# One kernel, four changes of order: first key products around a burst, gate rows earlier, gate dots held in place

## Chip, cores and metric

The kernel runs on one core of a Trainium2 chip, as one program. The metric is the device time of one execution in microseconds. The engines are named as in the profile: PE multiplies matrices, DVE and POOL are the two vector engines, ACT is the activation engine, and SP issues nearly all DMAs, from one queue that it works off in order.

## The reference, cut to what matters

Two layers update 1024 latent tokens (a 16 x 64 grid) of 1024 channels, beside 256 context tokens that share the weights. Each layer modulates its input, mixes it, gates the result and normalises it:

```
silu_c, silu_cc = silu(c), silu(c_ctx)
for i in range(2):
    shift, scale, gate     = split(silu_c  @ w_ada[i] + b_ada[i], 3)
    shift_c, scale_c, gate_c = split(silu_cc @ w_ada[i] + b_ada[i], 3)
    u, uc = h * (1 + scale) + shift, hc * (1 + scale_c) + shift_c
    y, yc = mixer_a(u, uc) if i == 0 else mixer_b(u, uc)
    h = layer_norm(ALPHA * h + gate * y, ln_g[i], ln_b[i])
    if i == 0:
        hc = layer_norm(ALPHA * hc + gate_c * yc, ln_g[i], ln_b[i])
return h
```

`mixer_a` (layer A here) is a windowed attention with 4 key heads for 16 query heads and rotary positions; `mixer_b` (layer B) attends in a neighbourhood of the grid with a learned bias. Both multiply the attention's output by a SiLU gate and by an output matrix. All is float32.

## The kernel before

A float32 product is made of three matmuls: both operands are split into a high and a low part (`uAh` and `uAl`, `wh` and `wl`), and high x high, high x low and low x high are added in PSUM. Channels are cut into 8 tiles of 128, counted by `kt`.

**Start.** For each channel tile, `mod_load` issues the tile's modulation weights (`wada`, two halves of 512 KB), attention weights and the tile of the input (`hraw`, 640 KB). `mod_rows` makes shift and scale of both modulation vectors as rows by 32 small matmuls (line 546, 16 for each half of `wada`) in the PSUM tile `kc`; ACT copies the rows out (line 553); `mod` turns them into columns by two matmuls (line 561) and DVE adds the bias (line 562, tile `adc`). `u_make` scales and shifts the three token chunks (two of 512 latent tokens, one of 256 context tokens; lines 580 to 584), ACT casts the high part (line 588, `uAh`) and DVE subtracts for the low part (line 589, `uAl`). `k_mm` then makes the key products, 12 of 512 columns in the tiles `kps` and 6 of 256 for the context in `kc` (lines 598 to 600), and `v_mm` the value products (lines 608 to 610). The loop over `kt` runs the modulation one tile ahead of the products. For `kt` of 2 and more the 32 row matmuls are one burst, second half first, held together by `tc.keep_in_program_order`; for tile 1 they are two separate halves.

**Order.** Instructions are written in a program order, and a scheduler then moves them on each engine by their priorities and readiness, except those held by `tc.keep_in_program_order`. `merge(att, fill, lead)` writes pieces of attention and pieces of other PE work in turn, by costs given as numbers.

**End of layer A.** The last attention pieces `att` are merged with output products of token tile 0 (`yA0`). Then `gate_rows` runs twice (`gts[:, 0]` for the latent and `gts[:, 1]` for the context gate): eight matmuls against the identity (line 377) that spread a gate column over all partitions into a large PSUM tile, of which two exist, and an ACT copy (line 378). The last six attention pieces follow, and the output tiles.

**Layer B's gate.** `gate_load` loads half a tile of gate weights into `gwB` (one buffer, 256 KB, line 1235) and `gate_dot` multiplies and sums it on DVE (line 1244), 16 times, for eight channel tiles. They are written one after the other into the sub-blocks of heads 1 to 8.

**Last stage.** For each of 8 token tiles `b`: load of `x` (three buffers, from the DRAM tensor `zdd`, layer A's output), `x * vecs[0] + vecs[1]` on POOL (lines 1340 and 1341), load of the attention output `og` for tile `b + 2`, the output products (`out_part`, lines 451 to 453; for tiles 0 and 1 only the last channel tile, read from `o7`, is left), then on DVE `z = y * g1` (line 1355), `z + x` (line 1356) and statistics (line 1357) by halves, the mean and variance (lines 459 and 460), the power -1/2 on POOL (line 461), two scalings on DVE (lines 1362 and 1364) and the store of the output (line 1365). `g1` is layer B's gate, made by `gate_rows` in the pass of tile 0.

Of the kernel before, what the change touches and what calls it, by code (L numbers as in the profile page):

```python
# [15 lines left out]
ALU = mybir.AluOpType  # L16
# [66 lines left out]
def build(tc, i, out):  # L83
# [452 lines left out]
    def mod_rows(kt):  # L536

        ws = wada.pop(kt)

        burst = kt > 1  # L540
        for n, hf in enumerate((1, 0) if burst else (0, 1)):
            for r in range(2):
                for x in range(2):
                    for kh in range(2):
                        g = 32 * (2 * x + kh)
                        ins = mm(
                            kc[g : g + 32, 512:640], sil[:, 4 * hf + 2 * r + kh, :], ws[hf][:, 2 * r + kh, x * P : (x + 1) * P],
                            start=n + r == 0, stop=n + r == 2, tile_position=(0, g),
                        )
                        if burst and n + r + x + kh:  # L550
                            tc.keep_in_program_order(ins)
        rows[kt] = pp.tile([P, P], F32, tag="rows", bufs=2, name="rows")
        ins = nc.scalar.copy(rows[kt], kc[:, 512:640])
        if kt == 2:

            tc.keep_in_program_order(ins)
# [34 lines left out]
    def k_mm(kt):  # L591
        for c, (t0, n) in enumerate(CHUNKS):
            for nt in range(2):
# [4 lines left out]
                mm(pt, hi[:, sl], rh, start=kt == 0 and (c < 2 or nt == 0), stop=False)  # L598
                mm(pt, lo[:, sl], rh, start=False, stop=False)
                mm(pt, hi[:, sl], rl, start=False, stop=kt == KT - 1 and (c < 2 or nt == 1))  # L600
# [13 lines left out]
    for kt in range(-1, KT + 1):  # L614
        if kt + 1 < KT:
            for n in range(3) if kt < 0 else (kt + 3,) if kt + 3 < KT else ():
                mod_load(n, upto[n])
                if n == 0:
                    w.split(2)
            mod_rows(kt + 1)  # L620
        if kt > 0:
            k_mm(kt - 1)
        if kt + 1 < KT:
            mod(kt + 1)
        if kt < 0:
# [4 lines left out]
        if kt < KT and kt >= 0:  # L630
            u_make(kt)
# [229 lines left out]
    for p in range(8):  # L861
# [13 lines left out]
        else:  # L875
# [22 lines left out]
            merge(att[:-6], fill, lead=1500.0)  # L898
            gts = up.tile([P, 2, D], F32, tag="l2", bufs=1, name="gates")
            for v in range(2):  # L900
                gate_rows(gts[:, v], dcol[:, 0:8, v])
# [335 lines left out]
    def gate_dot(j, x):  # L1237
# [6 lines left out]
        nc.vector.tensor_tensor_reduce(t, t, g, 0.5, acc if x else 0.0, ALU.mult, ALU.add, accum_out=acc)  # L1244
# [89 lines left out]
    for b in range(8):  # L1334
# [11 lines left out]
        parts = [slice(*c) for c in zip(cuts, cuts[1:])]  # L1346
        for sl in parts:
            out_part(y, sl, pairs, woB, range(KT) if b > 1 else (KT - 1,))
        if b == 0:
            g1 = ob.tile([P, D], F32, name="g1")  # L1350
            gate_rows(g1, dcol[:, 24:32, 0])
# [111 lines left out]
```

## Time and profile before

| what | value |
|---|---|
| median of 3 runs | 1423.81 us (1423.17 to 1426.17) |
| profiled execution, its own time | 1422.99 us |
| span of the profiled execution | 1421.2 us |
| granted TensorE clock, mean | 0.997 of full speed |
| PE busy | 1385.3 us (97%) |
| DVE busy | 980.0 us (69%) |
| ACT busy | 731.4 us (51%) |
| POOL busy | 626.2 us (44%) |

The profile shows one execution of the program; its times are counted from the start of the span, which ends 1.8 us short of the execution's own time. Busy time counts an engine's instructions; idle time ahead of one is put down to what ended it. A transfer that is issued from SP's queue starts no earlier than all issues ahead of it there.

### The profile page before, as it was taken

To read this page: it belongs to the slowest core of one execution; us is meant where nothing else is said; L and a number is where in the kernel's file an instruction comes from. 1 tells how busy PE (TensorE), PEld (TensorE's weight loads), DVE (VectorE), ACT (ScalarE), POOL (GpSimd) and SP (SyncE) were. 2 spreads that over 40 slices of the span, in tenths; PEclk is the share of its full clock that TensorE was granted. 3 is DMA by queue.
4 is the path that set the end of the run, shared out by engine and by line. 5 is a ranking of instruction groups with operands and counts; after the bars stand their busy time and mean duration, and the time that the engine had idled before them with its cause. 6 is when DMAs were issued, how large, how long until landed. Compare 5 with 4: busy or idle time off the path is not lost. (4 is left out here: it accounts for less than half of the span.)

```text
span 1421.2 us, 25164 instructions
## 1 busy us (share of the span) xinstructions
PE 1385.3 (97%) x8816; PEld 1215.2 (86%) x8816; DVE 980.0 (69%) x2220; ACT 731.4 (51%) x1560; POOL 626.2 (44%) x776
## 2 busy tenths in 40 slices
PE   8999999999999999999999999999999999999996
PEld 6988898888988888888898899888998899888885
DVE  4658887878888789566433766566665564659598
ACT  4337776676776778432222555454454454558200
POOL 0326676667666567233211333332233232325583
PEclk9999999999999999999999999999999999999998
DMA  9572114123222114443187575564555564476753
GB/s 377 181 224 85 54 57 126 53 79 92 79 73 64 57 60 146 127 135 133 62 260 218 156 214 165 143 189 137 179 150 172 150 185 146 137 209 185 181 149 107
DMA packets 128141, 202.39 MB, mean 142 GB/s; under 512 B 9744, under 2 KB 66448, under 8 KB 128016
## 3 DMA queue, kind: packets, MB, share of 16 engines
q1 hardware_dynamic: 127872, 200.78, 47.0%
q8 instruction: 70, 1.15, 0.3%
q14 instruction: 55, 0.45, 0.1%
q10 hardware_dynamic: 144, 0.01, 0.0%
HBM read 145.18 MB, written 55.57 MB: 141 GB/s over the span
## 5 line engine op out<-in xcount | busy, mean ns | idle before, releaser
L334 POOL TENSOR_SCALAR s_B<-s_B,rs_B 128x640 f32<-128x640 f32 (+1 forms) x128 | 103.2, 806 | 289.8 <-DVE rs_B L333 262.7
L212 PE MATMUL pj<-uBh,wh 128*128 128x512 f32 (+1 forms) x448 | 175.9, 393 | 0.0
L213 PE MATMUL pj<-uBl,wh 128*128 128x512 f32 (+1 forms) x448 | 170.3, 380 | 0.0
L214 PE MATMUL pj<-uBh,wl 128*128 128x512 f32 (+1 forms) x448 | 170.1, 380 | 0.0
L329 ACT ACTIVATE s_B<-s_B,m_B 128x640 f32<-128x640 f32 (+1 forms) x128 | 102.9, 804 | 126.1 <-DVE m_B L322 125.9
L329 ACT ACTIVATE s_A<-s_A,m_A 128x641 f32<-128x641 f32 (+2 forms) x160 | 119.5, 747 | 82.9 <-DVE m_A L322 60.1
L168 POOL TENSOR_TENSOR wl<-wr,wh 128x512 fp32r<-128x512 f32 x65 | 88.2, 1358 | 158.1 <-ACT wh L163 146.4
L334 POOL TENSOR_SCALAR s_A<-s_A,rs_A 128x640 f32<-128x640 f32 (+2 forms) x160 | 128.8, 805 | 65.0 <-DVE rs_A L333 58.9
L322 DVE CUSTOM_DVE_ANT_0 s_A<-S_A,msk,nsk 128x640 f32<-128x640 f32 (+2 forms) x160 | 123.5, 774 | 32.3 <-PE S_A L755 18.2
L347 DVE TENSOR_TENSOR pt_B<-T_B,pt_B 128x640 fp32r<-128x640 f32 (+1 forms) x128 | 100.9, 788 | 60.2 <-ACT pt_B L345 59.7
L212 PE MATMUL pj<-uAh,wh 128*128 128x512 f32 (+1 forms) x384 | 140.2, 365 | 0.8 <-DVE otmp L794 0.8
L213 PE MATMUL pj<-uAl,wh 128*128 128x512 f32 (+1 forms) x384 | 137.6, 358 | 0.0
L214 PE MATMUL pj<-uAh,wl 128*128 128x512 f32 (+1 forms) x384 | 137.2, 357 | 0.0
L347 DVE TENSOR_TENSOR ptl_A<-T_A,pth_A 128x640 fp32r<-128x640 f32 (+2 forms) x160 | 114.1, 713 | 16.8 <-PE pvA L783 10.5
L341 PE MATMUL T_A<-ident,s_A 128*128 128x128 f32 x672 | 100.9, 275 | 10.7 <-DVE m_A L322 5.3
L345 ACT CAST pt_B<-T_B 128x640 fp32r<-128x640 f32 (+1 forms) x128 | 84.4, 659 | 48.2 <-PE T_B L341 47.2
L341 PEld LDWEIGHTS T_A<-ident,s_A 128*128 128x128 f32 x672 | 77.3, 140 | 37.0 <-issue 10.1
L322 DVE CUSTOM_DVE_ANT_0 s_B<-S_B,bias 128x640 f32<-128x640 f32 (+1 forms) x128 | 100.2, 783 | 8.0 <-PE S_B L1092 7.0
L345 ACT CAST pth_A<-T_A 128x640 fp32r<-128x640 f32 (+2 forms) x160 | 96.3, 602 | 17.2 <-PE T_A L341 15.7
L214 PEld LDWEIGHTS pj<-uBh,wl 128*128 128x128 f32 x448 | 84.3, 188 | 16.6
L213 PEld LDWEIGHTS pj<-uBl,wh 128*128 128x128 f32 x448 | 84.7, 189 | 9.1
L341 PE MATMUL T_B<-ident,s_B 128*128 128x128 f32 x608 | 88.1, 274 | 4.2 <-DVE pt_B L347 2.3
(224 smaller groups left out, 3866.8 us busy)
## 6 DMA issues: line engine op xcount, KB each, us to landing
kB<-kdB SPq DMA_DIRECT2D x64, 320.0 KB, 5.4
gw<-in_wadaT SPq DMA_DIRECT2D x48, 256.0 KB, 2.8
vdB<-st SPq DMA_DIRECT2D x20, 512.0 KB, 3.6
vB<-vdB SPq DMA_DIRECT2D x16, 640.0 KB, 4.6
wada<-in_wadaC SPq DMA_DIRECT2D x16, 512.0 KB, 9.6
kdB<-st SPq DMA_DIRECT2D x16, 512.0 KB, 2.8
qdB<-st SPq DMA_DIRECT2D x16, 512.0 KB, 3.7
qB<-qdB SPq DMA_DIRECT2D x32, 256.0 KB, 4.8
```

The source lines that it names most:

```text
L168: e.tensor_tensor(lo, r, f32(hi), ALU.subtract)
L212: mm(pt[:, :n], hi[:, sl], rh, start=kt == 0, stop=False)
L213: mm(pt[:, :n], hi[:, sl], rl, start=False, stop=False)
L214: mm(pt[:, :n], lo[:, sl], rh, start=False, stop=kt == KT - 1)
L322: nc.vector.tensor_tensor_reduce(outp, sc, in1, scale, init if init is not None else 3e38, ALU.add, ALU.min, accum_out=s.m)
L329: nc.scalar.activation(s.t[:, :n], s.t[:, :n], AF.Exp, bias=s.m, scale=-1.0, accum_out=s.sum)
L334: nc.gpsimd.tensor_scalar(s.t[:, : s.w], s.t[:, : s.w], s.rs, 1.0, ALU.mult, ALU.mult)
L341: nc.tensor.transpose(tp[:, k * P : (k + 1) * P], s.t[:, src * P : (src + 1) * P], ident)
L345: nc.scalar.copy(pt.hi[:, :n, hl, :], tv)
L347: nc.vector.tensor_tensor(pt.lo[:, :n, hl, :], tv, f32(pt.hi[:, :n, hl, :]), ALU.subtract)
```

## The change

Four orders are changed, and no arithmetic:

- **Start.** The burst now begins with tile 1, whose 32 row matmuls run together, second half first, all held in program order. Tile 0's scaling is written ahead of tile 1's modulation; of tile 0's 18 key products the first 2 are written ahead of the burst, 4 behind it, and the other 12, the 6 context products among them, behind tile 1's line 561, the last two groups held in program order.
- **End of layer A.** `merge` gets all but the last eight attention pieces; the gate row of the latents, two attention pieces, the gate row of the context, and the last six pieces follow.
- **Layer B's gate.** The 16 dots are held in program order.
- **Last stage.** `gate_rows` is written ahead of tile 0's output products instead of behind them.

```diff
--- before.py
+++ after.py
@@ -537,7 +537,7 @@
 
         ws = wada.pop(kt)
 
-        burst = kt > 1
+        burst = kt > 0
         for n, hf in enumerate((1, 0) if burst else (0, 1)):
             for r in range(2):
                 for x in range(2):
@@ -547,7 +547,7 @@
                             kc[g : g + 32, 512:640], sil[:, 4 * hf + 2 * r + kh, :], ws[hf][:, 2 * r + kh, x * P : (x + 1) * P],
                             start=n + r == 0, stop=n + r == 2, tile_position=(0, g),
                         )
-                        if burst and n + r + x + kh:
+                        if kt == 1 or burst and n + r + x + kh:
                             tc.keep_in_program_order(ins)
         rows[kt] = pp.tile([P, P], F32, tag="rows", bufs=2, name="rows")
         ins = nc.scalar.copy(rows[kt], kc[:, 512:640])
@@ -588,16 +588,21 @@
             nc.scalar.copy(hi, x)
             nc.vector.tensor_tensor(lo, x, f32(hi), ALU.subtract)
 
-    def k_mm(kt):
+    def k_mm(kt, which=slice(None), fixed=False):
+        ps = []
         for c, (t0, n) in enumerate(CHUNKS):
             for nt in range(2):
                 hi, lo = w.got[KEYS[2 * (kt // 4) + nt]]
                 sl = slice((kt % 4) * P, (kt % 4 + 1) * P)
                 rh, rl = uA.at(kt, slice(t0, t0 + n))
                 pt = kps[c, nt] if c < 2 else kc[:, nt * C : nt * C + C]
-                mm(pt, hi[:, sl], rh, start=kt == 0 and (c < 2 or nt == 0), stop=False)
-                mm(pt, lo[:, sl], rh, start=False, stop=False)
-                mm(pt, hi[:, sl], rl, start=False, stop=kt == KT - 1 and (c < 2 or nt == 1))
+                ps.append((pt, hi[:, sl], rh, dict(start=kt == 0 and (c < 2 or nt == 0), stop=False)))
+                ps.append((pt, lo[:, sl], rh, dict(start=False, stop=False)))
+                ps.append((pt, hi[:, sl], rl, dict(start=False, stop=kt == KT - 1 and (c < 2 or nt == 1))))
+        for p in ps[which]:
+            ins = mm(*p[:3], **p[3])
+            if fixed:
+                tc.keep_in_program_order(ins)
 
     def v_mm(kt):
         hi, lo = w.got[VALUES[kt // 2]]
@@ -617,18 +622,27 @@
                 mod_load(n, upto[n])
                 if n == 0:
                     w.split(2)
+            if kt == 0:
+
+                u_make(0)
+                k_mm(0, slice(0, 2))
             mod_rows(kt + 1)
-        if kt > 0:
+            if kt == 0:
+                k_mm(0, slice(2, 6), True)
+        if kt > 1:
             k_mm(kt - 1)
         if kt + 1 < KT:
             mod(kt + 1)
+        if kt == 0:
+            k_mm(0, slice(6, None), True)
         if kt < 0:
 
             warm(vps[:, 0:512], 12)
         if kt > 0:
             v_mm(kt - 1)
         if kt < KT and kt >= 0:
-            u_make(kt)
+            if kt:
+                u_make(kt)
             w.split(upto[min(kt + 1, 7)])
     dma(ident, i["ident"])
     dma(lnc, i["lnc"])
@@ -895,10 +909,12 @@
             fill.append((0.0, og_first))
             for n in range(2 * KT):
                 fill.append((300.0, lambda n=n: out_part(yA0, HALVES[n // KT], oA0, woA, (n % KT,))))
-            merge(att[:-6], fill, lead=1500.0)
+
+            merge(att[:-8], fill, lead=1500.0)
             gts = up.tile([P, 2, D], F32, tag="l2", bufs=1, name="gates")
-            for v in range(2):
-                gate_rows(gts[:, v], dcol[:, 0:8, v])
+            gate_rows(gts[:, 0], dcol[:, 0:8, 0])
+            merge(att[-8:-6], [])
+            gate_rows(gts[:, 1], dcol[:, 0:8, 1])
             raw = og_load(1)
             merge(att[-6:], [])
     px_st.close()
@@ -1241,7 +1257,10 @@
             nc.scalar.activation(t, g, AF.Tanh, scale=0.5)
             nc.vector.scalar_tensor_tensor(g, t, 1.0, g, ALU.add, ALU.mult)
             return
-        nc.vector.tensor_tensor_reduce(t, t, g, 0.5, acc if x else 0.0, ALU.mult, ALU.add, accum_out=acc)
+
+        tc.keep_in_program_order(
+            nc.vector.tensor_tensor_reduce(t, t, g, 0.5, acc if x else 0.0, ALU.mult, ALU.add, accum_out=acc)
+        )
         if j == KT - 1 and x:
             nc.vector.tensor_tensor(dcol[:, 24:32, 0], dcol[:, 24:32, 0], bad[:, 40:48], ALU.add)
 
@@ -1344,11 +1363,12 @@
 
         cuts = (0, 512, 768, 1024) if b == 7 else (0, 512, D)
         parts = [slice(*c) for c in zip(cuts, cuts[1:])]
+        if b == 0:
+
+            g1 = ob.tile([P, D], F32, name="g1")
+            gate_rows(g1, dcol[:, 24:32, 0])
         for sl in parts:
             out_part(y, sl, pairs, woB, range(KT) if b > 1 else (KT - 1,))
-        if b == 0:
-            g1 = ob.tile([P, D], F32, name="g1")
-            gate_rows(g1, dcol[:, 24:32, 0])
         z = ob.tile([P, D], F32, tag="z", bufs=3, name="z")
         st = ob.tile([P, 3, 6], F32, tag="stat", bufs=2, name="stat")
         for j, sl in enumerate(parts):
```

**PE at the start.** The list begins with the first key product of tile 0 and shows the row matmuls of tile 1 (line 546; x8 here is x16 in the profile). In the names, `kp_0` and `kp_1` are the two key column groups, and `uAh_104`, `uAh_105` and `uAh_106` the first and second latent chunk and the context. Before:

```order
L598 MATMUL kp_0_142<-uAh_104,wh_160 128x512
L599 MATMUL kp_0_142<-uAh_104,wl_161 128x512
L546 MATMUL kc<-wada,sil 32x128 x8
L600 MATMUL kp_0_142<-uAl_107,wh_160 128x512
L598 MATMUL kp_1_143<-uAh_104,wh_164 128x512
L599 MATMUL kp_1_143<-uAh_104,wl_165 128x512
L600 MATMUL kp_1_143<-uAl_107,wh_164 128x512
L546 MATMUL kc<-wada,sil 32x128 x8
L598 MATMUL kp_0_144<-uAh_105,wh_160 128x512
L599 MATMUL kp_0_144<-uAh_105,wl_161 128x512
L561 MATMUL kc<-bad,rows 128x4
```

After (key products now stand in line 603):

```order
L603 MATMUL kp_0_142<-uAh_104,wh_160 128x512
L603 MATMUL kp_0_142<-uAh_104,wl_161 128x512
L546 MATMUL kc<-wada,sil 32x128 x16
L603 MATMUL kp_0_142<-uAl_107,wh_160 128x512
L603 MATMUL kp_1_143<-uAh_104,wh_164 128x512
L603 MATMUL kp_1_143<-uAh_104,wl_165 128x512
L603 MATMUL kp_1_143<-uAl_107,wh_164 128x512
L561 MATMUL kc<-bad,rows 128x4
L603 MATMUL kp_0_144<-uAh_105,wh_160 128x512
L603 MATMUL kp_0_144<-uAh_105,wl_161 128x512
L603 MATMUL kp_0_144<-uAl_108,wh_160 128x512
```

The second half of the row matmuls has moved up by four key products, and line 561 by two; behind these rows stand the rest of tile 0's 512-column products, and in the order after directly behind them its six context products, which in the order before follow only behind tile 2's burst.

**DVE at the gate dots.** Before, the dots stand in a row among the first head's softmax; here the fifth and sixth pair of loads (line 1244 is the dot and the read of its sum; line 347 makes `pt_B`, the transposed probabilities for PE):

```order
L333 RECIPROCAL rs_B_9343<-sum_B_9342 128x1
L1244 ISA gwB_1_10801,dcol<-gwB_1_10801,gsil,dcol 128x512
L1244 ISA dcol 128x1
L333 RECIPROCAL rs_B_9359<-sum_B_9358 128x1
L322 ISA s_B_9381,m_B_9382<-S_B_9376,bias_8695 128x640
L322 ISA m_B_9382 128x1
L333 RECIPROCAL rs_B_9384<-sum_B_9383 128x1
L1244 ISA gwB_0_10991,dcol<-gwB_0_10991,gsil 128x512
L1244 ISA dcol 128x1
L347 TENSOR_TENSOR pt_B_9394<-T_B_9395,pt_B_9394 128x4x128
```

After, the first dot stands here (line 1262), some 60 rows further on than the first before:

```order
L322 ISA s_B_9712,m_B_9713<-S_B_9707,bias_8696 128x640
L322 ISA m_B_9713 128x1
L996 SCALAR_TENSOR_TENSOR st<-pj_1_9646,st 128x512
L333 RECIPROCAL rs_B_9715<-sum_B_9714 128x1
L1154 TENSOR_TENSOR otmp<-pvB_2_9725,otmp 64x256 x2
L1262 ISA gwB_0_9656,dcol<-gwB_0_9656,gsil 128x512
L1262 ISA dcol 128x1
L347 TENSOR_TENSOR pt_B_9763<-T_B_9764,pt_B_9763 128x4x128
L168 TENSOR_TENSOR wl_9797<-wr_9554,wh_9796 128x512
```

The 16 dots are now spread over heads 1 to 8, behind an addition into `otmp` and ahead of a `pt_B` as here.

**SP in the last stage.** From tile 3's load of `x` on, before:

```order
L1336 DMA x<-zdd 128x1x1024
L1365 DMA out_h<-z 16x8x1024
L395 DMA og<-ogdB 128x4x128 x2
L395 DMA og<-ogdB 128x3x128 x2
L1336 DMA x<-zdd 128x1x1024
L1365 DMA out_h<-z 16x8x1024
L1336 DMA x<-zdd 128x1x1024
```

After:

```order
L395 DMA og<-ogdB 128x3x128
L1385 DMA out_h<-z 16x8x1024
L395 DMA og<-ogdB 128x3x128
L1355 DMA x<-zdd 128x1x1024
L395 DMA og<-ogdB 128x4x128 x2
L395 DMA og<-ogdB 128x3x128 x2
L1385 DMA out_h<-z 16x8x1024
L1355 DMA x<-zdd 128x1x1024 x2
```

The load of `x` for tile 3 (the first here) has moved behind tile 0's output, and that of tile 4 behind tile 1's output, where tile 5's stood already. On PE, tile 0's eight gate matmuls (line 377) have moved up by six products (lines 451 to 453).

## Rows read from the trace of the kernel before

**Rows 1.** The page's first part: engine, busy time, share of the span, instructions.

```profile
PE 1385.3 (97%) x8816; PEld 1215.2 (86%) x8816; DVE 980.0 (69%) x2220; ACT 731.4 (51%) x1560; POOL 626.2 (44%) x776
```

**Rows 2.** Stretches of the span (start:end, length, then for each engine its busy time and, in brackets, its instructions; granted TensorE clock as a share of full speed; DMA share; GB/s).

```profile
60.00:100.00 40.00, 40.00 (x266) 36.93 (x266) 26.59 (x41) 12.57 (x26) 16.59 (x13) 1.00 0.66 204
700.00:800.00 100.00, 98.57 (x591) 86.71 (x590) 41.16 (x98) 30.93 (x61) 19.15 (x19) 1.00 0.68 202
800.00:1200.00 400.00, 399.77 (x2691) 365.26 (x2690) 241.48 (x580) 199.58 (x412) 125.63 (x149) 1.00 0.58 167
1380.00:1421.00 41.00, 30.30 (x154) 25.30 (x152) 34.60 (x47) 0.00 (x0) 17.22 (x10) 0.91 0.41 109
```

**Rows 3.** The waits of PE, for the tile that waits and for what: us in total, times, longest us.

```profile
PE kp L598 <- ACT uAh L588: 2.5, 2, 1.9
PE T_B L341 <- DVE pt_B L347: 2.3, 5, 0.9
```

**Rows 4.** PE's timeline from 11 to 22 us: start, length, engine, line, operation, tile out<-in, shape, count, and in brackets the idle time ahead of it with what ended it.

```profile
11.34 0.50 PE L598 MATMUL kp<-uAh,wh 128*128 128x512 f32 x1 [1.93 <-ACT uAh L588]
...
12.00 0.65 PE L546 MATMUL kc<-wada,sil 128*32 128x128 f32 x16
...
13.14 0.40 PE L599 MATMUL kp<-uAh,wl 128*128 128x512 f32 x1
13.38 0.39 PE L600 MATMUL kp<-uAl,wh 128*128 128x512 f32 x1
13.70 0.64 PE L546 MATMUL kc<-wada,sil 128*32 128x128 f32 x16
...
16.73 0.50 PE L598 MATMUL kp<-uAh,wh 128*128 128x512 f32 x1 [0.58 <-ACT uAh L588]
...
19.00 1.08 PE L546 MATMUL kc<-wada,sil 128*32 128x128 f32 x32
...
20.93 0.28 PE L598 MATMUL kc<-uAh,wh 128*128 128x256 f32 x1
...
21.64 0.28 PE L561 MATMUL kc<-bad,rows 128*128 128x4 f32 x2
```

**Rows 5.** The same stretch on ACT (the casts of tile 1) and on DVE (tile 1's scale and shift).

```profile
16.08 1.43 ACT L588 CAST uAh<-hraw 128x512 fp32r<-128x512 f32 x3
...
15.16 0.16 DVE L562 TENSOR_TENSOR adc<-kc,bad 128x4 f32<-128x4 f32 x1 [2.21 <-PE kc L561]
```

**Rows 6.** The load of the modulation weights: first the DMA view of two short stretches with one such issue in each (4.0 to 4.5 us, tile 1's second half; 11.2 to 12.5 us, tile 3's second half): KB each, us from issue to landing; then SP's issue of the latter.

```profile
wada<-in_wadaC SPq DMA_DIRECT2D x1, 512.0 KB, 7.9
...
wada<-in_wadaC SPq DMA_DIRECT2D x1, 512.0 KB, 10.9
...
11.94 0.33 SPq L528 DMA_DIRECT2D wada<-in_wadaC  x1
```

**Rows 7.** The end of layer A's attention, 574 to 579 us, on PE, then ACT, then DVE.

```profile
574.38 1.04 PE L377 MATMUL gate<-ident,dcol 128*128 128x128 f32 x8
...
576.47 1.09 PE L377 MATMUL gate<-ident,dcol 128*128 128x128 f32 x8
...
578.65 0.50 PE L451 MATMUL yA<-woAh,og 128*128 128x512 f32 x1 [0.88 <-ACT gates L378]
...
577.59 1.01 ACT L378 COPY gates<-gate 128x1024 f32<-128x1024 f32 x1 [0.35 <-PE gate L377]
...
575.98 0.42 DVE L347 TENSOR_TENSOR ptl_A<-T_A,pth_A 128x256 fp32r<-128x256 f32 x1 [3.36 <-PE pvA L783]
```

**Rows 8.** Layer B's gate dots: of the view of the tile gwB the second halves' dots (durations min/median/max in ns, first and last start) and the total wait ahead of the dots (us, times); then the timeline from 786 to 793 us, DVE's rows and PE's.

```profile
L1244 DVE CUSTOM_DVE_ANT_0 gwB<-gwB,gsil,dcol x8: 732/751/1206, 765.9 to 836.1; 128x512 f32<-128x512 f32 x8
...
  DMA gwB<-in_wadaT: 16.5, 12
...
786.88 0.69 DVE L1244 CUSTOM_DVE_ANT_0 gwB<-gwB,gsil 128x512 f32<-128x512 f32 x1 [0.99 <-DMA gwB<-in_wadaT]
...
790.38 1.21 DVE L1244 CUSTOM_DVE_ANT_0 gwB<-gwB,gsil,dcol 128x512 f32<-128x512 f32 x1 [0.30 <-DMA gwB<-in_wadaT]
...
788.33 0.74 PE L341 MATMUL T_B<-ident,s_B 128*128 128x128 f32 x5 [0.94 <-DVE pt_B L347]
...
792.48 0.73 PE L341 MATMUL T_B<-ident,s_B 128*128 128x128 f32 x5 [0.49 <-DVE pt_B L347]
```

**Rows 9.** The last stage: PE's start on tile 0's products behind the gate; two DVE scalings of tiles of the same shape, one beside a POOL operation and one with POOL idle; SP's issues of tile 4's x and of tile 1's output; the DMA view of the stretch with tile 5's x (KB, us to landing); then pieces of the chain that ended last (start, length, what).

```profile
1342.61 0.50 PE L451 MATMUL yB<-woBh,og 128*128 128x512 f32 x1 [0.42 <-DVE z L1355]
...
1350.46 3.41 DVE L1364 SCALAR_TENSOR_TENSOR z<-z,rsd,vec 128x1024 f32<-128x1024 f32 x1
...
1408.33 1.29 DVE L1364 SCALAR_TENSOR_TENSOR z<-z,rsd,vec 128x1024 f32<-128x1024 f32 x1 [0.44 <-POOL rsd L461]
...
1358.30 0.55 SPq L1336 DMA_DIRECT2D x<-zdd  x1
1365.37 0.59 SPq L1365 DMA_DIRECT2D out_h<-z  x1
...
x<-zdd SPq DMA_DIRECT2D x1, 512.0 KB, 5.8
...
1368.70 2.37 POOL x L1340
...
1388.81 5.28 DMA x<-zdd
```

More of the change, by code (lines that the diff above doesn't have):

```diff
@@ L1346, in build @@
         parts = [slice(*c) for c in zip(cuts, cuts[1:])]
-        for sl in parts:
-            out_part(y, sl, pairs, woB, range(KT) if b > 1 else (KT - 1,))
         if b == 0:
@@ L1351, in build @@
             gate_rows(g1, dcol[:, 24:32, 0])
+        for sl in parts:
+            out_part(y, sl, pairs, woB, range(KT) if b > 1 else (KT - 1,))
         z = ob.tile([P, D], F32, tag="z", bufs=3, name="z")
```

## The prediction

> **What bounds the kernel now.** I read the page's first part, then stretches, PE's waits, and last the timelines of the four places that the change touches. PE is busy 1385.3 us [rows 1] of a span of 1421.2, so it sets the time nearly everywhere, and a microsecond is to be won only where PE stands idle or where the last stage ends later than PE does. The stretches show where that is: none from 60 to 100 us, 1.43 us from 700 to 800, 0.23 us in the 400 us from 800 to 1200, and 10.7 us from 1380 on [rows 2], where PE has finished and DVE and POOL bring the last tiles to their end. Two of PE's waits stand in the way of this change: 2.5 us for the first casts `uAh` and 2.3 us for `pt_B` [rows 3]. A gain that reaches PE at 16 us is kept at least up to 100 us, since PE has no idle time from 60 to 100 that could swallow it [rows 2]. At the very end it counts only if DVE's and POOL's chain moves with it.
>
> **Start.** No matmul is added or taken away. Before, PE makes the first half of tile 1's row matmuls at 12.00 us and the second at 13.70 [rows 4], DVE has shift and scale at 15.16, ACT begins the casts at 16.08 [rows 5], and PE waits 0.58 us until 16.73 for the first of them [rows 4]. Now the 32 matmuls stand together. A burst of 32 takes 1.01 us, from 19.00 to the next product; a 512-column product follows the one before it after 0.24 (13.14 to 13.38); a context product takes (21.64 - 20.93) / 6 = 0.12 [rows 4]. So: burst 12.0 to 13.0, four products and a switch to 14.05, line 561 there instead of at about 14.85 (its result came at 15.16 [rows 5], 0.3 later). The scale comes 0.8 us earlier, at 14.36, the first cast, which was ready just ahead of 16.73, at about 15.9. PE meanwhile has six products of tile 0 (6 x 0.24 = 1.4) and six context products (0.7), to about 16.3. The 0.58 us wait is covered, and one switch between row matmuls and products falls away: the two halves took 12.57 - 12.00 and 14.27 - 13.70, 1.14 us together by the starts of what follows, against 1.01, and each return to products costs a longer first one, so I count 0.3 to 0.5. Together about -1.0 to -1.2.
>
> The loads cap it. The burst begins with the half that is loaded last. That half is issued at about 4.1 and lands 7.9 later [rows 6], at 12.0: no margin. Should it come at 13.70, where it was used before [rows 4], a gain of 0.3 is left. Tile 3's second half is issued at 11.94 and takes 10.9 [rows 6], to 22.84, while its burst would start at about 22.7: 0.15 us go back. I take **-1.0**, range -0.3 to -1.4.
>
> **End of layer A.** Before, the eight gate matmuls start at 574.38 and the second eight at 576.47, after DVE's 575.98; ACT's second copy runs from 577.59 to 578.60, and the output product waits 0.88 us for it [rows 7]. That product needs the second large PSUM tile, so it still follows the second copy. Now two attention pieces stand between the two, and PE has four 256-column products and two transposes more to do before that product: 4 x 0.12 [rows 4] and some 0.2, about 0.7 us, which hides most of the 0.88. Against it stands that the attention ahead is merged with fewer pieces in reserve, so a wait for DVE or POOL may show up earlier. I take **-0.5**; the ends are -0.9, all of the wait and no more, and +0.7, a new wait of the size of the one removed less what is won.
>
> **Gate dots.** Before, the 16 dots follow one another from about 762 to 836 us, and DVE, which works in order, waits 16.5 us ahead of them for the loads of `gwB` [rows 8]. Two such places reach PE: the dot at 786.88, which waited 0.99, and the one at 790.38, which ran 1.21; behind them `pt_B` is late and PE waits 0.94 and 0.49 [rows 8], together the 1.43 that PE lost from 700 to 800 [rows 2]. Now each dot stands in a sub-block of its own and its load some two sub-blocks ahead, so DVE should find it loaded. The two waits go: **-1.3**, at most -1.43. What the change adds is that each of the 16 dots, 0.69 or 0.75 long, stands directly ahead of a `pt_B`. The nearest rows: dots run up to 836.1 [rows 8], and PE loses 0.23 us in all from 800 to 1200 [rows 2]. The dots from 800 to 836 therefore cost PE nothing or almost nothing, and I count the new ones at zero too; the other end is a rival below. The loads are the same 16, spread over heads, and free SP.
>
> **Last stage.** Gate matmuls move up by six products, 6 x 0.24 = 1.4 us. PE's wait of 0.42 on DVE's first `z` [rows 9] goes, and DVE starts 1.4 us sooner. But PE does not end the kernel there: the chain runs through POOL's work on `x` at 1368.70, tile 4's, and the load of tile 7's `x` at 1388.81 [rows 9]. In SP's queue, tile 4's `x` was issued at 1358.30, ahead of tile 1's output at 1365.37 [rows 9]; with tile 5's 5.8 us to landing it was there at 1364.1, 4.6 us ahead of POOL. Now it is issued only behind that output. With DVE 1.4 us sooner the output goes at about 1364.0, 0.6 for its issue, and tile 5's load, the nearest, took 5.8; the one on the chain 5.3. That makes 1369.9 with the shorter time (1370.4 with the longer), against 1368.70: POOL, and with it the end, is **1.2** late, while PE's gain of the three earlier places moves all of this stage alike. Bounds: -0.4, if POOL is not the last here and 0.42 of PE's wait counts, and +3, if a DVE step falls behind POOL as well.
>
> **Sum.** -1.0 - 0.5 - 1.3 + 1.2 = -1.6 us. Against the profiled execution's 1422.99 that is 1421.4. That execution is 0.82 us below the median of the three runs, 1423.81; the forecast for the median is 1423.81 - 1.6 = **1422.2**.
>
> **Rivals.** *The last stage gives nothing back.* DVE is early by more than 1.4 us, or POOL waits for DVE in any case, so that tile 4's `x` is in time. Then -2.8, and up to -1.4 more if the whole lead of the gate reaches the end: 1419.6 to 1421.0. For it: the three gains each have a wait of PE that is seen in the rows. Against it: the 1.2 comes from an order in SP's queue that is fixed, and tile 4's load has only 1365.37 - 1358.30 = 7.1 us less room than before.
>
> *The dots hold PE up (slower than before).* Each dot delays a `pt_B` by 0.7, and PE's output products of that sub-block wait for it as they did at 788.33. DVE sits idle a good part of the time from 800 to 1200 (241 of 400 us busy [rows 2]), which speaks against it; that 0.94 of wait arose behind a single dot speaks for it [rows 8]. At 0.4 each, 16 x 0.4 = 6.4 on top of the sum: +4.8, 1428.6. It decides the sign from 1.6 / 16 = 0.1 us for each dot.
>
> *DVE falls behind POOL in the last stage.* The scaling of line 1364 took 3.41 us beside POOL's work on `x` and 1.29 with POOL idle [rows 9], so one such meeting costs 2.1 us. POOL's and DVE's meetings all shift when DVE starts 1.4 sooner and tile 3's and 4's `x` come later. One more meeting on the chain gives -1.6 + 2.1 = +0.5: 1424.3; one fewer gives -3.7: 1420.1, inside the first rival. The Trainium skill, "SBUF — State Buffer", section "SBUF: two separate sides", states it as a rule: a DVE operation with two SBUF inputs and a POOL operation need one shared pair of ports, and whoever starts first keeps it for the whole instruction. By that rule the cost of a meeting is all of the rest of POOL's operation, not a share; the two durations agree with it.
>
> *The change does less than it says.* `wada`'s half lands at 13.7 and the gate rows of layer A only move their wait: -0.3 - 1.3 + 1.2 = -0.4, 1423.4.
>
> **Chances.** The forecast 0.42; nothing given back 0.32; dots 0.10; one more meeting 0.11; less than it says 0.05. A measurement of this kernel tells a change from none from about 0.2% on, 2.85 us: below 1420.96 or above 1426.66. The forecast, the additional meeting and the last case lie within it, 0.58, less 0.01 for a run of them above. The first rival is almost all below, 0.32. The dots and that rest are above, 0.11. The range leaves out the dots, and little at the other end: 1419.4, just below the first rival's lower end, to 1425.5, the meeting with 1.2 more.
>
> **What the next profile would show.** Start: row matmuls x32 at about 12.0, the scale about 0.8 us sooner, no wait of PE for `uAh` behind 11.34. If the burst starts later than 12.3, the load binds. Layer A: an output product behind the second gate copy with a wait under 0.4. Dots: no wait of DVE for `gwB` and none of PE for `pt_B` near 788 and 792; PE waits for `pt_B` in heads 1 to 8 beyond 1 us in all would be the dots' price. Last stage: PE's first product of tile 2 without a wait, but POOL waiting for a load of `x` ahead of tile 4's line 1359; if POOL doesn't wait there, the 1.2 is wrong, and the kernel is faster than I say. If PE's total idle time ahead of 1300 us falls by less than 2 us, the three gains are wrong.

## The result and the profile after

The changed kernel takes 1427.90 us (median of 10 runs, 1425.45 to 1429.88) against 1423.89 for the kernel before (10 runs): ratio 1.0026, 95% interval 1.0017 to 1.0036, or 3.7 us slower (2.4 to 5.1). Its profiled execution took 1427.96 us with a span of 1425.9, 4.7 more than before.

Stretches of the changed kernel, columns as in [rows 2]:

```profile
520.00:580.00 60.00, 56.26 (x366) 49.05 (x366) 47.89 (x108) 46.43 (x99) 36.44 (x54) 1.00 0.36 115
700.00:800.00 100.00, 100.00 (x599) 88.19 (x598) 36.31 (x83) 30.81 (x61) 19.41 (x20) 1.00 0.60 180
800.00:1200.00 400.00, 398.23 (x2678) 363.49 (x2677) 246.37 (x591) 197.86 (x408) 126.04 (x147) 1.00 0.59 172
1380.00:1425.80 45.80, 30.88 (x156) 25.76 (x154) 34.57 (x47) 0.00 (x0) 19.92 (x10) 0.88 0.37 97
```

And one stretch of the kernel before that [rows 2] don't have:

```profile
520.00:580.00 60.00, 58.05 (x378) 50.72 (x377) 48.18 (x114) 47.03 (x102) 38.11 (x55) 1.00 0.36 116
```

Idle time of PE is length less busy time. From 60 to 100 us there is none, as before. From 700 to 800 us it is gone (1.43 before, [rows 2]), but 1.77 us have come from 800 to 1200 (0.23 before), and 520 to 580 has 3.74 where it had 1.95. Busy time in all is the same, 1385.3 us. PE's last product begins 0.58 us later than before (1410.60 against 1410.02), so the rest of the 4.7, some 4.1 us, lies behind PE in this execution: from the last product to the end of the span it is 15.3 us, before 11.2. Ahead of 1300 us PE is idle for 23.9 us, before 22.7; a fall of less than 2 us was the prediction's sign that its three gains are wrong.

PE's timeline at the start, columns as in [rows 4]:

```profile
11.42 0.50 PE L603 MATMUL kp<-uAh,wh 128*128 128x512 f32 x1 [1.80 <-ACT uAh L588]
...
12.13 1.08 PE L546 MATMUL kc<-wada,sil 128*32 128x128 f32 x32
...
14.18 0.28 PE L561 MATMUL kc<-bad,rows 128*128 128x4 f32 x2
...
16.50 0.40 PE L603 MATMUL kp<-uAh,wh 128*128 128x512 f32 x1
...
18.43 1.08 PE L546 MATMUL kc<-wada,sil 128*32 128x128 f32 x32
```

The burst is one, the modulation's matmul (line 561) stands at 14.18, and the first product of tile 1 at 16.50 waits for nothing, where [rows 4] had 0.58. Tile 2's burst starts 0.57 earlier, with one product of 0.24 less and six of 0.12 more done by then. PE has run 529 products by 60 us instead of 521.

PE's timeline at the end of layer A:

```profile
532.75 0.74 PE L341 MATMUL T_A<-ident,s_A 128*128 128x128 f32 x5 [0.94 <-DVE m_A L322]
...
553.05 0.74 PE L341 MATMUL T_A<-ident,s_A 128*128 128x128 f32 x5 [0.71 <-POOL s_A L334]
...
555.95 0.74 PE L341 MATMUL T_A<-ident,s_A 128*128 128x128 f32 x5 [0.50 <-DVE m_A L322]
...
579.83 0.50 PE L451 MATMUL yA<-woAh,og 128*128 128x512 f32 x1 [0.28 <-ACT gates L378]
```

The wait behind the second gate copy fell from 0.88 [rows 7] to 0.28. But waits of 0.5 to 0.9 stand 24 to 47 us ahead of it.

A gate dot, the `pt_B` behind it, and PE's new waits for `pt_B`; DVE's rows first, then PE's:

```profile
983.25 1.45 DVE L1262 CUSTOM_DVE_ANT_0 gwB<-gwB,gsil,dcol 128x512 f32<-128x512 f32 x1
...
984.63 0.81 DVE L347 TENSOR_TENSOR pt_B<-T_B,pt_B 128x640 fp32r<-128x640 f32 x1
...
985.59 0.74 PE L341 MATMUL T_B<-ident,s_B 128*128 128x128 f32 x5 [0.49 <-DVE pt_B L347]
...
1049.20 0.74 PE L341 MATMUL T_B<-ident,s_B 128*128 128x128 f32 x5 [0.36 <-DVE pt_B L347]
```

No dot waits for its load any more. One dot took 1.45 us where the others of its kind take 0.74, and the `pt_B` behind it kept PE waiting 0.49. The other wait has no dot next to it.

The last stage: POOL's rows, then SP's issues of `x` for tile 3 and for tiles 4 and 5:

```profile
1360.83 1.52 POOL L461 TENSOR_TENSOR rsd<-rsd,half 128x1 f32<-128x1 f32 x1 [3.21 <-DVE rsd L460]
1364.36 2.40 POOL L1359 TENSOR_TENSOR x<-x,vec 128x1024 f32<-128x1024 f32 x1 [2.00 <-DMA x<-zdd]
...
1371.38 2.81 POOL L1359 TENSOR_TENSOR x<-x,vec 128x1024 f32<-128x1024 f32 x1 [0.77 <-DMA x<-zdd]
...
1356.73 1.71 SPq L1355 DMA_DIRECT2D x<-zdd  x1
...
1364.46 2.25 SPq L1355 DMA_DIRECT2D x<-zdd  x2
```

POOL waits 3.21 us for DVE ahead of tile 1's power (line 461), then 2.00 and 0.77 for loads of `x`. Tile 3's load was issued at about 1357.9 behind tile 0's store, where before it went at 1346.29, and tile 4's at 1364.46 instead of 1358.30 [rows 9].

### The profile page after: what moved, and what is told of

The parts are those of the page before. It is cut to its first block, busy times and chain, and to the rows that moved or that the text cites. A ratio compares the mean times of both kernels' runs of the same rounds, so it can differ in the third digit from the quotient of the medians.

```text
span 1425.9 us, 25160 instructions
## 1 busy us (share of the span) xinstructions
PE 1385.3 (97%) x8816; PEld 1215.5 (85%) x8816; DVE 979.6 (69%) x2220; ACT 730.7 (51%) x1560; POOL 627.9 (44%) x776
## 5 line engine op out<-in xcount | busy, mean ns | idle before, releaser
L347 DVE TENSOR_TENSOR ptl_A<-T_A,pth_A 128x640 fp32r<-128x640 f32 (+2 forms) x160 | 114.2, 714 | 15.3 <-PE pvA L797 7.4
L212 PEld LDWEIGHTS pj<-uBh,wh 128*128 128x128 f32 x448 | 84.5, 189 | 9.1
```

Source lines behind the costliest of these rows:

```text
L212: mm(pt[:, :n], hi[:, sl], rh, start=kt == 0, stop=False)
L347: nc.vector.tensor_tensor(pt.lo[:, :n, hl, :], tv, f32(pt.hi[:, :n, hl, :]), ALU.subtract)
```

## The experiments

Each was timed beside the kernel before on the same chip, 8 to 11 runs each. Microseconds are the ratio less one, times the median of the kernel before beside it (1424.86 to 1425.71), with the 95% interval.

**The four parts alone.** Each kernel is the one before with one part of the diff.

> Only the start is changed. Theory 1 (the four parts add up, each as far as its own stage shows it after the change): about -0.7 us, which is what the full change shows at 60 us, kept to the end: some 1423.2. Theory 2 (a gain at the start is swallowed later, because waits of layer A follow DVE and POOL): 0 within 0.3 us.

Measured: 0.9996, -0.6 us (-1.9 to +0.7). Neither theory is excluded by the time alone.

> Only the end of layer A is changed. Theory 1: slower by 1.5 to 2 us: the new waits for scores and probabilities between 532 and 560 us cost about 2.6, the wait behind the second gate copy falls from 0.9 to 0.3. Theory 2 (these waits come from the start's shift and not from the earlier end of the merge): -0.6 us, no wait of more than 0.5 us between 532 and 560.

Measured: 1.0024, +3.4 us (+2.3 to +4.7). PE's waits between 520 and 562 us are the ones of the full change.

> Only the 16 gate dots are held in place. Theory 1: about 0 (-1.4 from 786 to 793 us, +1.5 from new waits of 0.2 to 0.7 us in heads 2 to 8). Theory 2 (the dots are what slows the kernel): +2 us or more. My prediction's own step: -1.3.

Measured: 0.9991, -1.3 us (-2.6 to -0.1). In its profile the 1.43 us from 700 to 800 are gone, and PE waits for `pt_B` 0.20, 0.49 and 0.23 us between 947 and 1048. A further wait of 0.80 for scores at 885 is no price of the dots: with the last stage's part alone one of 0.43 stands there too.

> Only the gate rows of the last stage are moved ahead. Theory 1 (tile 3's and 4's loads of x stand behind output stores in SP's queue and POOL waits for them): +3 to +4.5 us, POOL waiting 1 us or more for tiles 3 and 4, PE's last product no later than before. Theory 2 (the loss in the full change comes from the phase in which PE reaches the last stage, after the other three parts): within 1 us of before. My prediction's own step: +1.2.

Measured: 1.0011, +1.6 us (+0.4 to +2.8). The four add up to +3.1; the full change has +3.7. Each has an interval of about 1.3 us either way, so these runs show no action of the parts on each other and would miss a small one. The end of layer A is the largest.

**The end of layer A, taken apart.** First the cut of the merge without moving the gate rows apart:

```diff
-            merge(att[:-6], fill, lead=1500.0)
+            merge(att[:-8], fill, lead=1500.0)
+            merge(att[-8:-6], [])
```

> The kernel before with the merge at the end of layer A cut at eight attention pieces instead of six, and nothing else: the two pieces follow, then both gate rows together, as before. Theory 1 (the cut is what costs: with fewer attention pieces for the same output work, merge writes the output work, and DVE's splits of its weights, earlier between the pieces, and DVE's score maxima come late all the way back to 520 us): slower by 3 us or more, with the waits for m_A between 520 and 562 us and also the 0.9 us behind the second gate copy. Theory 2 (the gate rows apart are what costs): within 0.7 us of before.

Measured: 1.0012, +1.7 us (+0.4 to +3.0). In its profile, ACT's rows, then DVE's, then PE's:

```profile
530.31 0.62 ACT L367 CAST woAh<-wor 128x512 fp32r<-128x512 f32 x1 [1.30 <-DMA wor<-in_wAo]
530.83 0.83 ACT L329 ACTIVATE s_A<-s_A,m_A 128x641 f32<-128x641 f32 x1
...
531.78 0.16 DVE L333 RECIPROCAL rs_A<-sum_A 128x1 f32<-128x1 f32 x1 [1.00 <-ACT s_A L329]
531.90 0.88 DVE L322 CUSTOM_DVE_ANT_0 s_A<-S_A,msk,nsk 128x640 f32<-128x640 f32 x1
...
532.94 0.74 PE L341 MATMUL T_A<-ident,s_A 128*128 128x128 f32 x5 [0.97 <-DVE m_A L322]
```

And ACT in the kernel before, the exponential of the same place and the cast that waits for its load:

```profile
530.43 0.83 ACT L329 ACTIVATE s_A<-s_A,m_A 128x641 f32<-128x641 f32 x1
...
533.85 0.62 ACT L367 CAST woAh<-wor 128x512 fp32r<-128x512 f32 x1 [0.74 <-DMA wor<-in_wAo]
```

After the cut, a cast of output weights (line 367) stands ahead of the exponential, and waits 1.30 us for its DMA. ACT works in order: the exponential's maximum is there at 529.10, and it still begins only behind the cast, at 530.83. DVE's reciprocal (line 333) waits 1.00 for that exponential, the score maximum behind it is late, and PE waits 0.97 for the maximum. In the kernel before, the exponential goes first and the cast that waits comes 3 us later. The cut gives `merge` fewer attention pieces for the same fill, so all fill, the weight casts with it, is written earlier between them, tens of microseconds ahead of the place that the change is about. At this place PE's wait grows from 0.45 to 0.97, which is a part of the 2.9 us that the cut costs by the profile (below). The other new waits, the largest 0.73 at 553.3 for POOL and 0.51 at 556.2, were not taken apart; ahead of the first, splits of output weights (line 368) run on DVE (1.84 us from 550.47) and on POOL (1.32 from 550.45). No run holds such a step back alone: that the cut costs is shown by times, that it does so through these steps is read from the profile.

Then the gate rows apart without the cut, as a piece of no cost inside the merge:

```diff
-            merge(att[:-6], fill, lead=1500.0)
-            for v in range(2):
-                gate_rows(gts[:, v], dcol[:, 0:8, v])
+            first = (0.0, lambda: gate_rows(gts[:, 0], dcol[:, 0:8, 0]), 0)
+            merge(att[:-8] + [first] + att[-8:-6], fill, lead=1500.0)
+            gate_rows(gts[:, 1], dcol[:, 0:8, 1])
```

> The kernel before with the first gate row written two attention pieces earlier, as a piece of no cost inside the merge, so that the merge's other pieces keep their order; only the gate rows move. Theory 1: -0.4 to -0.9 us: the wait behind the second gate copy falls from 0.9 to 0.3 or less, and the waits between 520 and 562 stay as before (0.5 us). Theory 2: slower by 2 us or more.

Measured: 0.9987, -1.9 us (-3.4 to -0.3). PE's waits from 515 to 590 for the score maximum, and the two groups of gate matmuls:

```profile
PE T_A L341 <- DVE m_A L322: 1.7, 2, 1.2
...
572.75 1.04 PE L377 MATMUL gate<-ident,dcol 128*128 128x128 f32 x8
...
575.70 1.04 PE L377 MATMUL gate<-ident,dcol 128*128 128x128 f32 x8
```

The maxima cost 1.7 us, as in the kernel before, where the same two waits are 1.2 and 0.45, and no output product waits for a gate copy. So the idea of the part was good, and the cut that came with it was what cost. The stretch from 500 to 700 us, columns as in [rows 2], first of the kernel before:

```profile
500.00:700.00 200.00, 196.60 (x1060) 165.79 (x1059) 144.12 (x327) 96.87 (x197) 83.66 (x117) 1.00 0.34 112
```

of the part alone:

```profile
500.00:700.00 200.00, 194.50 (x1053) 164.11 (x1052) 145.32 (x329) 97.54 (x199) 83.77 (x120) 1.00 0.34 112
```

of the cut alone:

```profile
500.00:700.00 200.00, 193.68 (x1046) 163.39 (x1045) 143.68 (x325) 95.63 (x194) 82.98 (x117) 1.00 0.34 112
```

and of the gate rows apart alone:

```profile
500.00:700.00 200.00, 196.99 (x1062) 165.76 (x1061) 144.18 (x327) 97.19 (x198) 83.83 (x117) 1.00 0.34 112
```

PE idles 3.40, 5.50, 6.32 and 3.01 us. By the profiles the cut costs 2.9 and the gate rows apart give 0.4 without it, 0.8 with it.

**The last stage, first try.** I took the loads of `x` behind output stores for the cause, as the prediction has it, and wrote each load right behind the last reading of its buffer.

```diff
+            if b + 3 < 8:
+                x_load(b + 3)
             mv, rs = ln_stats(ob, st[:, : len(parts)])
```

> The gate rows of the last stage ahead, as in the change, and tile b+3's load of x written right behind tile b's last reading of its buffer, so that on SP it stands ahead of the output store; POOL's order changes with it (tile 3's two steps follow tile 2's). Theory 1 (the loads behind output stores cost): 2 to 4 us less than with the gate rows alone, so -0.5 to -2 against before, and POOL waits for no load of tiles 3 and 4. Theory 2 (the meetings of DVE and POOL cost, not the loads): still slower than before by 1 us or more.

Measured: 1.0014, +2.0 us (+0.6 to +3.3).

> The kernel before with only the loads of x written earlier, as in the run with the gate rows. Theory 1: -0.5 to 0 us, since before has tile 3's and 4's loads in time and only those of tiles 6 and 7 are waited for, which are bound by their buffer and not by the stores. Theory 2: 0, or slower by 1 us, if the order of POOL's steps decides.

Measured: 1.0030, +4.3 us (+2.9 to +5.8). Both say little of the cause. The earlier loads wait on SP for their buffers (22.0 and 19.8 us in all) with loads of `og` behind them. POOL's order moved too: in the first, tile 3's two steps stand ahead of tile 1's power, and POOL then waits for the loads of tiles 4 to 7 (1.79, 1.92, 3.42 and 2.09 us).

**The stores on another queue.** This takes the stores out of the loads' way. By the profiles it leaves DVE's order as it is, but not all of POOL's, as shown below:

```diff
-            dma(grid_rows(out, b)[:, :, sl], z[:, sl])
+            nc.scalar.dma_start(grid_rows(out, b)[:, :, sl], z[:, sl])
```

> Only the last stage's gate rows ahead, as in the run with that part alone, and the output stores issued from ACT's queue, which has nothing else to do there; POOL's, DVE's and PE's orders are as in that run, and on SP the loads of x no longer stand behind stores. Theory 1 (tile 3's and 4's loads behind stores in SP's queue cost): -0.5 to -1.5 us against before, so 2 to 3 us less than the gate rows alone, and POOL waits for neither load. Theory 2 (DVE's and POOL's meetings cost, and the gate's place decides them): +1 us or more against before.

Measured: 1.0010, +1.4 us (+0.1 to +2.7).

> The kernel before with only the output stores on ACT's queue. Theory 1: -0.5 to 0 us, since before has the loads of tiles 3 and 4 in time; later loads are bound by their buffers. Theory 2: 0.

Measured: 0.9990, -1.4 us (-2.7 to -0.1). So the gate rows ahead cost 2.8 us here with no load behind a store: there is a cause beside mine. The first of the two in profile, POOL's rows, then DVE's:

```profile
1360.08 1.53 POOL L461 TENSOR_TENSOR rsd<-rsd,half 128x1 f32<-128x1 f32 x1 [3.20 <-DVE rsd L460]
1361.58 2.39 POOL L1340 TENSOR_TENSOR x<-x,vec 128x1024 f32<-128x1024 f32 x1
...
1373.43 0.55 POOL L461 TENSOR_TENSOR rsd<-rsd,half 128x1 f32<-128x1 f32 x1
...
1374.02 3.42 DVE L1365 SCALAR_TENSOR_TENSOR z<-z,rsd,vec 128x1024 f32<-128x1024 f32 x1 [2.21 <-POOL rsd L461]
```

POOL waits 3.20 us ahead of tile 1's power, and only then begins tile 3's `x`; tile 2's power comes at 1373.43, behind the steps for tiles 3 and 4, and DVE's scaling of tile 2 waits 2.21 for it, then runs 3.42 beside POOL's next step. In the kernel before, tile 3's first step stands ahead of tile 1's power and fills the time in which POOL waits.

This pair does not clear the loads in the change itself, because POOL's order is another one here: with the stores on ACT's queue tile 4's two steps stand ahead of tile 2's power, with the gate ahead and without. With the stores on SP's queue they stand behind it. POOL, then DVE, in the run of the last stage's part alone:

```profile
1365.59 2.39 POOL L1340 TENSOR_TENSOR x<-x,vec 128x1024 f32<-128x1024 f32 x1 [3.00 <-DMA x<-zdd]
...
1371.28 0.55 POOL L461 TENSOR_TENSOR rsd<-rsd,half 128x1 f32<-128x1 f32 x1
1371.80 2.40 POOL L1340 TENSOR_TENSOR x<-x,vec 128x1024 f32<-128x1024 f32 x1
...
1371.87 3.42 DVE L1365 SCALAR_TENSOR_TENSOR z<-z,rsd,vec 128x1024 f32<-128x1024 f32 x1 [2.21 <-POOL rsd L461]
```

and POOL in the kernel before:

```profile
1367.18 1.52 POOL L461 TENSOR_TENSOR rsd<-rsd,half 128x1 f32<-128x1 f32 x1 [2.92 <-DVE rsd L460]
1368.68 2.39 POOL L1340 TENSOR_TENSOR x<-x,vec 128x1024 f32<-128x1024 f32 x1
```

In the part alone POOL waits 3.00 us for tile 3's load, tile 2's power comes right behind tile 3's steps, and DVE waits 2.21 for it, from 1369.66 on. My estimate from these rows: without the 3.00 the power would be done at 1368.8, and DVE would not wait. So there the late load can make the wait by itself. What follows takes POOL's order apart with the stores on ACT's queue only.

**POOL's order.** Two first kernels moved more than one step. In the first the gate stays, the stores go on ACT's queue, and two steps are held in program order, which puts tile 1's power ahead but tile 4's steps ahead of tile 3's as well:

```diff
+        if b == 3:
+            tc.keep_in_program_order(ins)
...
+        mv, rs = ln_stats(ob, st[:, : len(parts)], b == 1)
```

> The stores on ACT's queue and the gate where it was before; only POOL's order differs from that run: tile 1's power is held ahead of tile 3's first step on x. Theory 3 (POOL's order is the cost): +2 to +3 us against the stores alone, so +0.5 to +1.5 against before, POOL waiting about 3 us ahead of the power. Theory 4 (the earlier gate and DVE's order are the cost): as the stores alone, -1.4.

Measured: 1.0009, +1.3 us (+0.1 to +2.6).

In the second the gate rows are ahead, the stores on ACT's queue, and tile 3's load and first step are written ahead of tile 1's statistics, which moved both its steps:

```diff
+        if b == 1:
+            x_begin(3)
         mv, rs = ln_stats(ob, st[:, : len(parts)])
```

> The stores on ACT's queue and the gate rows ahead, with tile 3's two steps on x ahead of tile 1's power on POOL. Theory 3: -1 to -2 us against before, as the stores alone or a little better. Theory 4: +1 to +1.5, as with the gate rows ahead and the stores on ACT's queue.

Measured: 0.9992, -1.1 us (-2.6 to +0.3). Both are as theory 3 has it. The last two have the stores on ACT's queue too, so that they stand beside the pair above. They hold all of POOL's steps in program order, and by the profiles DVE keeps the order of the run of that pair with the same place of the gate. Of the two, the first takes the late order with the gate where it was, the second the early order with the gate rows ahead. Both orders have tile 4's steps ahead of tile 2's power, as the pair above has. The exchange, from the early order to the late, as a list of steps (`x3 *` is line 1340 for tile 3, `x3 +` line 1341):

```diff
-POOL: x2 *, x2 +, x3 *, power 1, x3 +, x4 *, x4 +, power 2
+POOL: x2 *, x2 +, power 1, x3 *, x3 +, x4 *, x4 +, power 2
```

> The gate where it was, the stores on ACT's queue, and of all orders only POOL's changed by one place: tile 1's power ahead of tile 3's first step on x. Theory 3 (POOL's order is the cost): +2 to +3 us against the stores alone, so +0.6 to +1.6 against before. Theory 4 (the earlier gate and DVE's order are the cost): as the stores alone, -1.4.

Measured: 1.0014, +2.0 us (+0.9 to +3.3), with the gate where it was.

```profile
1359.94 1.52 POOL L461 TENSOR_TENSOR rsd<-rsd,half 128x1 f32<-128x1 f32 x1 [3.21 <-DVE rsd L460]
1361.43 11.90 POOL L1343 TENSOR_TENSOR x<-x,vec 128x1024 f32<-128x1024 f32 x4
1373.30 0.54 POOL L461 TENSOR_TENSOR rsd<-rsd,half 128x1 f32<-128x1 f32 x1
...
1373.87 3.41 DVE L1377 SCALAR_TENSOR_TENSOR z<-z,rsd,vec 128x1024 f32<-128x1024 f32 x1 [2.19 <-POOL rsd L461]
```

> The gate rows ahead, the stores on ACT's queue, and POOL's order as before has it: tile 3's first step on x ahead of tile 1's power. Theory 3: 2 to 3 us less than with POOL's order of the change, so about -1.4 against before. Theory 4: +1.4, as with POOL's order of the change.

Measured: 0.9990, -1.4 us (-2.8 to 0), with the gate rows ahead.

```profile
1351.59 8.64 POOL L1343 TENSOR_TENSOR x<-x,vec 128x1024 f32<-128x1024 f32 x3
1361.64 1.52 POOL L461 TENSOR_TENSOR rsd<-rsd,half 128x1 f32<-128x1 f32 x1 [1.41 <-DVE rsd L460]
1363.13 8.54 POOL L1343 TENSOR_TENSOR x<-x,vec 128x1024 f32<-128x1024 f32 x3
1371.63 1.53 POOL L461 TENSOR_TENSOR rsd<-rsd,half 128x1 f32<-128x1 f32 x1
...
1373.27 1.27 DVE L1378 SCALAR_TENSOR_TENSOR z<-z,rsd,vec 128x1024 f32<-128x1024 f32 x1
```

Both fences show POOL's rows and then DVE's scaling of tile 2. With the power ahead, POOL idles 3.21 and has four steps left, 11.90 us, before tile 2's power, and DVE's scaling begins at 1373.87 and takes 3.41. With tile 3's first step ahead, POOL idles 1.41 and has three steps left, 8.54, and the scaling takes 1.27. Late order +2.0 and +1.4, early order -1.4 and -1.4, whether the gate is ahead or not: with the stores there the exchange is the cost, 2.8 to 3.4 us, and the gate's place by itself is worth nothing that these runs can tell. With the stores on SP's queue, as in the change, no run has the exchange without the late load or the late load without the exchange.

**Versions that keep what gains.** First the start, the dots and the gate rows apart without the cut, the last stage as before; then the last stage's part with them; then the first of these with the stores on ACT's queue; and the second with those stores and `x_begin(3)` written ahead of tile 1's statistics as above.

> The start and the gate dots as in the change, the gate rows of layer A apart but without the cut of the merge, the last stage as before. Theory 1 (the parts add): -0.6 for the start, -0.7 for the dots, -0.8 for the gate rows: about -2 us, 0.9986 of before. Theory 2 (gains are swallowed at the last stage, whose end is set by DVE and POOL): within 0.7 us.

Measured: 0.9987, -1.9 us (-3.1 to -0.6). The three alone have -0.6, -1.3 and -1.9, in sum -3.8; the intervals allow both.

> As the run before it, and the last stage's gate rows ahead as in the change: the full change without the cut of the merge. Theory 1: +1.6 us above the run without the last part, so about -0.5 against before, and 3 us or more below the full change. Theory 2: as slow as the full change, +3 to +4.

Measured: 0.9997, -0.4 us (-1.7 to +0.9). Without the cut the full change is no longer slower.

> Start, dots and the gate rows of layer A without the cut, the last stage as before with the stores on ACT's queue. If the parts add: -2 and -1.4, 0.9976 of before. If the last stage's end is set by DVE and POOL whatever PE does: no better than -2.

Measured: 0.9980, -2.8 us (-4.0 to -1.6).

> As the run before it, with the last stage's gate rows ahead and tile 3's two steps on x ahead of tile 1's power. Theory 3: as the run before it or up to 1 us faster. Theory 4: 2 to 3 us slower than the run before it.

Measured: 0.9974, -3.7 us (-5.0 to -2.4), the lowest of all, and faster than both kernels; its interval overlaps that of the run before it. Its stretches:

```profile
520.00:580.00 60.00, 58.84 (x381) 51.21 (x381) 47.85 (x111) 46.95 (x101) 37.98 (x54) 1.00 0.36 115
700.00:800.00 100.00, 100.00 (x603) 88.36 (x602) 36.47 (x83) 31.54 (x62) 20.03 (x20) 1.00 0.60 177
800.00:1200.00 400.00, 398.98 (x2684) 364.24 (x2683) 248.41 (x598) 200.34 (x414) 126.98 (x148) 1.00 0.60 172
```

From 520 to 580 PE idles 1.16 us (before 1.95), from 700 to 800 not at all, and from 800 to 1200 1.02: the dots' price is still there.

## Why the prediction was wrong

**Start: right.** Forecast -1.0. By 60 us PE is eight products ahead, 8 x 0.12 = 1.0, the wait of 0.58 is gone and PE waited for no load of a burst. The time alone, -0.6 (-1.9 to +0.7), agrees but would not show it.

**End of layer A: the step that failed.** I forecast -0.5 and bounded a loss by +0.7, "a new wait of the size of the one removed less what is won". The wait behind the copy did what I said. But the part also cut the merge. I did write that a wait might show up earlier with fewer pieces in reserve, and sized it at one wait, as if the cut were a local edit. It moves the fill along the whole last piece of attention; on ACT's queue, which I never read there, it puts a weight cast with a late DMA ahead of an exponential, which is one of six places where PE then waits longer. Alone the part costs +3.4 us (+2.3 to +4.7). Of the two halves the cut alone has +1.7 and the gate rows apart alone -1.9, which add up to -0.2 and not to +3.4. By PE's idle time from 500 to 700 us the cut costs 2.9, the part 2.1 and the gate rows apart -0.4, and these do add up to within half a microsecond; so the times differ from the profiles by 1.2 to 1.5 us each, and what these are stays open. That the cut is the loss holds either way: the full change with the cut has +3.7, without it -0.4.

**Gate dots: right, with a price I set at zero.** Forecast -1.3; measured -1.3 (-2.6 to -0.1). The profile shows 1.43 gained and 0.5 to 0.9 paid for `pt_B`, so that the time meets the forecast so closely is luck. The price is far from the 6.4 of the rival, and that the changed kernel's 1427.9 lies near that rival's 1428.6 is chance. That before lost 0.23 us from 800 to 1200 did show that a dot ahead of a `pt_B` is cheap, but not that all sixteen are free.

**Last stage: right size, mechanism not settled.** Forecast +1.2 for tile 4's load behind tile 1's store; measured +1.6 (+0.4 to +2.8). That these are near is in part luck. In the part alone POOL does not wait for tile 4's load at all (in the full change 0.77), but 3.00 us for tile 3's, issued behind tile 0's store, which my sum left out. And POOL's order changed, of which no row of the prediction tells; I costed only SP's. With the stores on ACT's queue, where no load stands behind a store, that exchange alone costs 2.8 to 3.4 us. With them on SP's queue, as in the change, the late load and the exchange come together, and which of them costs there stays open.

The meeting of DVE and POOL that I gave 2.1 us as a rival shows in the pair that holds POOL's order: tile 2's scaling takes 3.41 in one order and 1.27 in the other. The Trainium skill, "SBUF — State Buffer", section "SBUF: two separate sides", has the loser of the shared ports wait for the whole of the other's instruction; these two rows agree. In the changed kernel such a meeting does not simply come on top: tile 2's scaling takes 1.28 us (at 1370.64) where the kernel before has 3.33 (at 1368.82), and tile 3's 3.41 (at 1383.69) where before has 1.28 (at 1381.55).

**Sum.** -0.6 + 3.4 - 1.3 + 1.6 = +3.1, measured +3.7. The merge's cut carries most of the loss: without it the same four changes have -0.4. The last stage's part adds 1.5 there (-0.4 against -1.9) and 1.6 alone, by tile 3's late load, POOL's exchange or both. The last version has neither and is 3.7 us faster than before, but the kernel with only the stores moved to ACT's queue has 1.4 of that.

One reading was too sharp. From PE's last product to the end, the profile of before has 11.2 us, while profiles of kernels with the same last stage have 11.8 to 13.1; a last stage that DVE and POOL decide is not known to a microsecond from one execution.

## What to carry to other kernels

Where a planner spreads filling work over a list, shortening the list moves all of the filling: compare every engine's order from the list's first piece on, not at the place of the edit. In a stage where two engines wait for each other in turn, cost the order of the engine that works in order and idles there: with the stores on ACT's queue, one short step put ahead of a long one that was ready cost about 3 us. Read the orders of a test kernel as well: the scheduler moved POOL's steps when only the stores' queue was changed. And when several parts move at once, time each alone before the sum is believed; here the dots gained, two parts lost, and the start's gain shows only in the profile.

## What the runs showed of the hardware

The kernel with the output stores on ACT's queue instead of SP's takes 1.4 us less (0.1 to 2.7). POOL takes tile 4's steps ahead of tile 2's power there, so it is not shown that the queue alone gives this.

The same gate dot takes 0.74 us or, in one case, 1.45, about twice, without any wait ahead of it. A split of weights (line 168) runs on POOL beside that one, from 982.40 to 984.15; that this is the reason was not tried.
